# Where the columns and the weights of a matmul lie in SBUF, modulo 256 bytes, and three 128-column passes ahead of one tile

## The chip, the cores and the metric

The kernel runs on one core of one Trainium2 chip. The metric is device microseconds of one execution. Three executions of the kernel before took 2719.71, 2716.47 and 2715.73 us; the median is 2716.47 us.

## The reference

Two layers over 272 tokens (16 learned ones ahead of 256 of the input), width 2048. Cut to its matrix products:

```python
u = rmsnorm(h, norm_mix[0]);  h = h + ssd_mixer(u, ...)        # u @ in_proj, scan, g @ out_proj
h = h + swiglu(rmsnorm(h, norm_ffn[0]), gate_up[0], down[0])
kv = rmsnorm(h, kv_norm) @ w_kv
u = rmsnorm(h, norm_mix[1]);  h = h + stick_breaking_attention(u, w_q, k, v, w_o)
h = h + swiglu(rmsnorm(h, norm_ffn[1]), gate_up[1], down[1])
return rmsnorm(h, final_norm)[:, 16:]

def swiglu(u, w_gate_up, w_down):
    gu = u @ w_gate_up
    return (silu(gu[..., :5632]) * gu[..., 5632:]) @ w_down
```

Layer 0 and the shared keys and values need all 272 tokens; the queries and all that follows them need 256.

## The kernel before

**Tiling.** Activations stand transposed: 128 features on the partitions, tokens along the free axis (272, or 256 from the queries on). A projection is made one output tile at a time: 128 output features, accumulated in one PSUM bank over the K tiles of its input (16 for `u`, `ukv`, `uq` and `ob`; 8 for `y`, the half of the mixer's output that one call takes; 44 for `hid`). For each K tile the weights are a 128x128 block, loaded into TensorE, and the tokens are streamed past it.

**Three products per K tile.** Weights and activations are each split into a high part that the fp32r format holds and a low rest. `mac` (L107 to L112) issues for each K tile `wh*xh` (L110), `wh*xl` (L111) and `wl*xh` (L112); each is one weight load and one pass of 272 or 256 columns. The load for the next pass runs while the columns of the present one are read. So what is read from SBUF at the same time is always the columns of one pass and the weights of the pass behind it.

**How the weights come.** `load` (L91) fetches eight K tiles of a weight matrix (512 KB) into one of five `raw` buffers on SP's queue; `halves` (L99) makes `hi` on ScalarE (L101, five buffers) and `lo` on VectorE (L103, four buffers). `project` runs one output tile through that, `project_block` several output tiles in turn for each eight K tiles. Where an output tile is finished, VectorE reads it from PSUM (`times`, `residual`), and `split_scaled` writes the high and low part of the next input.

**Where things lie.** The tiles come from pools that fill each partition from low to high addresses. As the built program has it, in bytes of a partition:

| tile | starts at | modulo 256 | order inside | bytes from one K tile to the next |
|---|---|---|---|---|
| `hi`, `lo` (all buffers) | 81920 ... 114688 | 0 | K tile, 128 columns | 512 |
| `u`, `ukv` (272 columns) | 26624 | 0 | K tile, (high, low), token | 2176 (128 modulo 256) |
| `u` of layer 1 (256 columns) | 26624 | 0 | the same | 2048 (0 modulo 256) |
| `y` (272) | 132672, 150080 | 64 | the same | 2176 |
| `hid` of layer 0 (272) | 126400 | 192 | the same | 2176 |
| `hid` of layer 1, `uq`, `ob` (256) | 126400, 126400, 159168 | 192 | the same | 2048 |

In what follows, the distance of a pass is the address of the weights that are loaded meanwhile less the address of its columns, modulo 256. With 256 columns it is the same in every pass: 0 where the columns are those of `u`, 64 where they are those of `hid`, `uq` or `ob`. With 272 columns a high part is 1088 bytes long (64 modulo 256) and a K tile 2176, so the distance goes through 0, 192, 0, 128, 64, 128 over two K tiles of `u`, and through 64, 0, 64, 192, 128, 192 over those of `hid`.

**Stages**, in us from the span's start: `w_first`, `w_dt` and the mixer (272 columns, with the scan's small matmuls spread among the projections by `pump`) to 749; gate and up of layer 0 (272) to 1280; down (272) to 1543; keys, values and queries with the attention between (272 and 256) to 1863; `w_o` (256) to 1955; gate and up of layer 1 (`u`, 256) to 2462; down (`hid`, 256) to 2702; the final norm.

Of the kernel before, what the change touches and what calls it, by code (L numbers as in the profile page):

```python
# [29 lines left out]
WC = 8  # L30
# [7 lines left out]
WAKE = 10  # L38
RAW = 5
# [3 lines left out]
def trunk(tc, a, out):  # L43
# [3 lines left out]
    with tc.tile_pool(name="const", bufs=1) as cp, \  # L47
# [36 lines left out]
        uid = [0]  # L84

# [12 lines left out]

        def halves(raw, n, m=P):  # L99
            hi = wp.tile([P, WC, P], F32R, tag="hi", name=nm("hi"), bufs=5)  # L100
            S.copy(hi[:, :n, :m], raw[:, :n, :m])  # L101
            lo = wp.tile([P, WC, P], F32R, tag="lo", name=nm("lo"), bufs=4)
            V.tensor_tensor(out=lo[:, :n, :m], in0=raw[:, :n, :m],  # L103
                            in1=hi[:, :n, :m].bitcast(F32), op=ALU.subtract)
            return hi, lo

        def mac(ps, hi, lo, j, x, k, first, last, m=P):  # L107
            n = x.shape[-1]
            wh, wl, xh, xl = hi[:, j, :m], lo[:, j, :m], x[:, k, 0, :], x[:, k, 1, :]
            PE.matmul(ps[:, :n], wh, xh, start=first, stop=False)  # L110
            PE.matmul(ps[:, :n], wh, xl, start=False, stop=False)  # L111
            PE.matmul(ps[:, :n], wl, xh, start=False, stop=last)  # L112

        def project(src, x, m=P, o=None, then=None):
            K = x.shape[1]
            if o is None:
                o = pp.tile([P, 512], F32, tag="pp", name=nm("pp"))
            o = o[:m]
            for k0 in range(0, K, WC):
                c = min(WC, K - k0)  # L120
                if k0 % LC == 0:
                    raw = load(src, k0, min(LC, K - k0), m)
                hi, lo = halves(raw[:, k0 % LC:], c, m)
                for j in range(c):
                    mac(o, hi, lo, j, x, k0 + j, k0 + j == 0, k0 + j == K - 1, m)
                if k0 == 0 and then:
                    then()
            return o

        def project_block(srcs, x, then=None):  # L130
            K = x.shape[1]
            pss = [pp.tile([P, 512], F32, tag="pp", name=nm("pp")) for _ in srcs]
            for k0 in range(0, K, WC):
# [16 lines left out]
        def split_scaled(dst, k, src, gcol):  # L150
            S.activation(dst[:, k, 0, :], src, AF.Identity, scale=gcol)
            V.scalar_tensor_tensor(out=dst[:, k, 1, :], in0=src, scalar=gcol,
                                   in1=dst[:, k, 0, :].bitcast(F32),
                                   op0=ALU.mult, op1=ALU.subtract)
# [33 lines left out]
        u = upool.tile([P, KD, 2, T], F32R, tag="u", name="u0")  # L188
# [23 lines left out]
        with tc.tile_pool(name="ssd0", bufs=1) as q0, \  # L212
# [12 lines left out]
            ybuf = [q0.tile([P, 2 * GT, 2, T], F32R, name=f"y{i}") for i in range(2)]  # L225
# [113 lines left out]
            def ssd_scan(g, bc, xc, zs):  # L339
# [37 lines left out]
                ef = q2.tile([P, GT, T - OQ], F32, tag="ef", name=nm("ef"))  # L377
# [36 lines left out]
                ga = sp.tile([P, T], F32, tag="ga", name=nm("ga"))  # L414
# [20 lines left out]
                rg = sp.tile([P, T], F32, tag="rg", name=nm("rg"))  # L435
                rstd(rg, ga, DI // G)
                yield
                yb = ybuf[g // 2 % 2][:, g % 2 * GT:(g % 2 + 1) * GT]
                for j in range(GT):
# [3 lines left out]
                    S.copy(yb[:, j, 0, :], zs[:, j, :])  # L443
                    V.tensor_tensor(out=yb[:, j, 1, :], in0=zs[:, j, :], in1=yb[:, j, 0, :].bitcast(F32),
# [23 lines left out]
            u = upool.tile([P, KD, 2, T], F32R, tag="u", name="u1")  # L468
            out_project(6, u)


        def ffn(layer, u, t0, finish):
            n = T - t0
            with tc.tile_pool(name=f"ffn{layer}", bufs=1) as fp, \
                    tc.tile_pool(name=f"fft{layer}", bufs=2) as ft:
                hid = fp.tile([P, KF, 2, n], F32R, name=f"hid{layer}")
# [4 lines left out]
                for m in range(KF):  # L481
                    gt = ft.tile([P, n], F32, tag="gt", name=nm("gt"))
                    times(gt, pre.pop(0) if pre else project(gu[m], u), r)
# [4 lines left out]
                    S.copy(hid[:, m, 0, :], ut)  # L488
                    V.tensor_tensor(out=hid[:, m, 1, :], in0=ut, in1=hid[:, m, 0, :].bitcast(F32),
# [8 lines left out]
        def finish0(m, ps):  # L498
            if m == 0:
                ukv[0] = upool.tile([P, KD, 2, T], F32R, tag="u", name="ukv")  # L500
# [8 lines left out]
        with tc.tile_pool(name="att1", bufs=1) as b1p, \  # L509
                tc.tile_pool(name="att2", bufs=2) as b2p, \  # L510
                tc.tile_pool(name="psa", bufs=3, space=PSUM) as pap:
            uq = b1p.tile([P, KD, 2, SEQ], F32R, name="uq")
            for k in range(KD):
                split_scaled(uq, k, h[:, k, META:], gam[:, 1, k:k + 1])
            ob = b1p.tile([P, KD, 2, SEQ], F32R, name="ob")
# [17 lines left out]
            def attend(m, kT, vT, qT):  # L533
# [39 lines left out]
                S.copy(ob[:, m, 0, :], po[:, :SEQ])  # L573
                V.tensor_tensor(out=ob[:, m, 1, :], in0=po[:, :SEQ], in1=ob[:, m, 0, :].bitcast(F32),
# [21 lines left out]
            u = upool.tile([P, KD, 2, SEQ], F32R, tag="u", name="u2")  # L596
# [29 lines left out]
        diag = cp.tile([P, 2, P], F32, name="diag")  # L626
# [88 lines left out]
```

## Time and profile before

| | us |
|---|---|
| median of three runs | 2716.47 |
| the profiled execution, its own time | 2715.76 |
| its span (first to last instruction) | 2714.0 |
| VectorE busy in the span | 1605.6 |
| ScalarE busy | 1307.1 |
| DMA q1, share of 16 engines | 57.3% |
| granted TensorE clock, mean | 0.998 |

The profiled execution's own time is 1.8 us over its span and 0.7 us under the median. TensorE's busy time says little by itself, since a pass is recorded from its start to the end of its drain and neighbours overlap: a 272-column pass is shown with 287 ns, while the next one starts some 125 ns after it. The pace is read from the starts of the passes, or from their number in a stretch without pauses.

### The profile page before, as it was taken

Reading aid. Unit: us, or ns where it says so; the run is one execution under the profiler, and the core shown is the slowest. Engines: PE = TensorE matmul, PEld = TensorE weight load, DVE = VectorE, ACT = ScalarE, POOL = GpSimd, SP = SyncE. Lnnn points to the kernel's source line nnn. Section 1 sums busy time; section 2 is a strip of 40 time slices with the busy share of each in tenths; the row PEclk is TensorE's granted clock in tenths of the full one; section 3 lists DMA queues with packets and bytes.
Section 4 is the critical chain, followed back from the end, with each engine's and each line's share of the span. In section 5 each row is a group of like instructions: output and inputs, shape, how many; then the busy total and the mean of one; then the engine's idle time right before and its main releaser. Section 6 shows DMA issues by size and latency. Waiting matters only on the chain.

```text
span 2714.0 us, 52235 instructions
## 1 busy us (share of the span) xinstructions
PE 2700.6 (100%) x22112; PEld 2685.5 (99%) x22112; DVE 1605.6 (59%) x2220; ACT 1307.1 (48%) x1792; POOL 5.5 (0%) x22
## 2 busy tenths in 40 slices
PE   9999999999999999999999999999999999999998
PEld 9999999999999999999999999999999999999998
DVE  8777767668755555555444655555655555554554
ACT  7766566645544444444343544444544444443443
POOL 0000000000000000000000000000000000000000
PEclk9999999999999999999999999999999999999999
DMA  6755555654555555555555555555665666565664
GB/s 224 225 177 177 177 171 177 180 170 155 173 177 174 176 172 177 174 176 175 172 175 174 173 172 158 156 156 162 193 181 184 182 186 181 185 182 177 204 195 138
DMA packets 156235, 481.24 MB, mean 177 GB/s; under 512 B 18720, under 2 KB 39776, under 8 KB 156000
## 3 DMA queue, kind: packets, MB, share of 16 engines
q1 hardware_dynamic: 155712, 477.62, 57.3%
q8 instruction: 173, 2.83, 0.4%
q14 instruction: 62, 0.51, 0.1%
q10 hardware_dynamic: 288, 0.28, 0.0%
HBM read 475.67 MB, written 2.17 MB: 176 GB/s over the span
## 4 chain that ended last, share of the span: by engine, by line
PE 99%; DVE 0%; DMA 0%; ACT 0%; issue 0%; DVEq 0%; SPq 0%; ACTq 0%
PE pp L110 31%; PE pp L112 31%; PE pp L111 31%; PE py L422 1%; PE py L424 1%; PE pt L349 0%; PE po L571 0%; PE po L570 0%; PE psc L545 0%; PE pr L170 0%; DMA et<-cumD 0%; DMA raw<-w_first 0%; PE pe L110 0%; PE pe L112 0%; PE pe L111 0%; DVE o L642 0%
## 5 line engine op out<-in xcount | busy, mean ns | idle before, releaser
L101 ACT CAST hi<-raw 128x1024 fp32r<-128x1024 f32 (+1 forms) x899 | 928.5, 1034 | 1231.2 <-PE pp L111 994.9
L103 DVE TENSOR_TENSOR lo<-raw,hi 128x1024 fp32r<-128x1024 f32 (+1 forms) x899 | 1076.4, 1199 | 502.3 <-PE pp L112 280.9
L110 PE MATMUL pp<-u,hi 128*128 128x272 f32 (+1 forms) x4064 | 1166.7, 287 | 0.5 <-ACT hi L101 0.5
L112 PE MATMUL pp<-u,lo 128*128 128x272 f32 (+1 forms) x4064 | 1165.3, 287 | 0.2 <-DVE lo L103 0.2
L111 PE MATMUL pp<-u,hi 128*128 128x272 f32 (+1 forms) x4064 | 1163.2, 286 | 0.0
L111 PEld LDWEIGHTS pp<-u,hi 128*128 128x128 f32 x4064 | 775.3, 191 | 0.2
L110 PEld LDWEIGHTS pp<-u,hi 128*128 128x128 f32 x4064 | 769.4, 189 | 1.2 <-ACT hi L101 0.7
L112 PEld LDWEIGHTS pp<-u,lo 128*128 128x128 f32 x4064 | 768.9, 189 | 1.2 <-DVE lo L103 0.8
L110 PE MATMUL pp<-hid,hi 128*128 128x272 f32 (+1 forms) x1408 | 397.0, 282 | 0.0
L112 PE MATMUL pp<-hid,lo 128*128 128x272 f32 (+1 forms) x1408 | 396.4, 282 | 0.0
L111 PE MATMUL pp<-hid,hi 128*128 128x272 f32 (+1 forms) x1408 | 396.1, 281 | 0.0
L111 PEld LDWEIGHTS pp<-hid,hi 128*128 128x128 f32 x1408 | 265.3, 188 | 0.0
L110 PEld LDWEIGHTS pp<-hid,hi 128*128 128x128 f32 x1408 | 264.6, 188 | 0.0
L112 PEld LDWEIGHTS pp<-hid,lo 128*128 128x128 f32 x1408 | 264.3, 188 | 0.0
L110 PE MATMUL pp<-ukv,hi 128*128 128x272 f32 x512 | 149.0, 291 | 0.0
L110 PE MATMUL pp<-y,hi 128*128 128x272 f32 x512 | 148.7, 290 | 0.0
L112 PE MATMUL pp<-ukv,lo 128*128 128x272 f32 x512 | 147.6, 288 | 0.0
L111 PE MATMUL pp<-y,hi 128*128 128x272 f32 x512 | 147.4, 288 | 0.0
L111 PE MATMUL pp<-ukv,hi 128*128 128x272 f32 x512 | 147.4, 288 | 0.0
L112 PE MATMUL pp<-y,lo 128*128 128x272 f32 x512 | 147.1, 287 | 0.0
L145 DVE TENSOR_TENSOR gt<-pp,rB 128x272 f32<-128x272 f32 (+1 forms) x88 | 38.1, 433 | 145.0 <-PE pp L112 145.0
L145 DVE TENSOR_TENSOR ut<-pp,rB 128x272 f32<-128x272 f32 (+1 forms) x88 | 38.1, 433 | 144.0 <-PE pp L112 144.0
(218 smaller groups left out, 2602.2 us busy)
## 6 DMA issues: line engine op xcount, KB each, us to landing
raw<-w_gu SPq DMA_DIRECT2D x352, 512.0 KB, 3.6
raw<-w_down SPq DMA_DIRECT2D x160, 512.0 KB, 3.8
raw<-w_in SPq DMA_DIRECT2D x152, 512.0 KB, 3.6
raw<-w_out SPq DMA_DIRECT2D x64, 512.0 KB, 3.7
raw<-w_kv SPq DMA_DIRECT2D x64, 512.0 KB, 3.6
raw<-w_q SPq DMA_DIRECT2D x32, 512.0 KB, 3.6
raw<-w_o SPq DMA_DIRECT2D x32, 512.0 KB, 3.6
raw<-w_down SPq DMA_DIRECT2D x32, 256.0 KB, 2.6
```

Source lines behind the costliest of these rows:

```text
L101: S.copy(hi[:, :n, :m], raw[:, :n, :m])
L103: V.tensor_tensor(out=lo[:, :n, :m], in0=raw[:, :n, :m], in1=hi[:, :n, :m].bitcast(F32), op=ALU.subtract)
L110: PE.matmul(ps[:, :n], wh, xh, start=first, stop=False)
L111: PE.matmul(ps[:, :n], wh, xl, start=False, stop=False)
L112: PE.matmul(ps[:, :n], wl, xh, start=False, stop=last)
L145: V.tensor_tensor(out=dst, in0=ps[:, :r.shape[-1]], in1=r, op=ALU.mult)
L422: PE.matmul(py[i * HD:(i + 1) * HD, c0:c1], xd[b][:, 2 * j + i, :], gm[b][:, 2 * j + i, :], start=b < 2, stop=b != 1)
L424: PE.matmul(py[:, T:T + T - OQ], xw[:, 2 * j:2 * j + 2, :], cb[:, OQ:T], start=True, stop=True)
```

## The change

**Layout of the columns.** `pair` replaces the tile of (K tile, high or low, token) by one tile that holds all low parts and behind them, after a gap, all high parts; `PAD` sets what lies ahead. **Layout of the weights.** `hi` and `lo` are tiles of 1152 columns; with 272 tokens the K tiles of weights lie 144 columns (576 bytes, 64 modulo 256) apart, with 256 tokens 128 columns, and then `lo` begins 48 columns in. **Order in `mac`:** `wh*xl`, `wh*xh`, `wl*xh`. **Room:** `ef`, `ga` and `rg` have one buffer in place of two; `diag` stands in another pool. **Short passes:** ahead of the gate tile `m == 2` of layer 1, `syncopate` issues three passes of 128 columns into a PSUM bank that nothing reads.

As the built program has it, `hi` now starts at 64 and `lo` at 128 modulo 256 (192 more where it begins 48 columns in, so 64), the low parts of `u`, `y`, `uq`, `ob` and `hid` at 0, their high parts at 64 with 272 columns and at 0 with 256. The distance is 64 in every pass but some hundred of `w_first`.

```diff
+PAD = {"u": 0, "u2": 0, "y": 48, "uq": 16, "ob": 0, "hid": (16, 16)}
...
+        for tag, bufs in (("raw", RAW), ("hi", 5)):
+            wp.tile([P, 8 * P if tag == "raw" else WC * 144], F32 if tag == "raw" else F32R, tag=tag, name=f"{tag}_", bufs=bufs)
+        wp.tile([P, 16], F32, name="gap")
...
         def halves(raw, n, m=P):
-            hi = wp.tile([P, WC, P], F32R, tag="hi", name=nm("hi"), bufs=5)
+            st = STEP[0]
+            hi = wp.tile([P, WC * 144], F32R, tag="hi", name=nm("hi"), bufs=5)
+            hi = hi[:, :WC * st].rearrange("p (k c) -> p k c", c=st)
+            lo = wp.tile([P, WC * 144], F32R, tag="lo", name=nm("lo"), bufs=4)
+            o = 0 if st > P else 48
+            lo = lo[:, o:o + WC * st].rearrange("p (k c) -> p k c", c=st)
             S.copy(hi[:, :n, :m], raw[:, :n, :m])
-            lo = wp.tile([P, WC, P], F32R, tag="lo", name=nm("lo"), bufs=4)
...
+        def pair(pool, K, n, pad, gap, **kw):
+            t = pool.tile([P, pad + 2 * K * n + gap], F32R, **kw)
+            return [t[:, o:o + K * n].rearrange("p (k t) -> p k t", t=n) for o in (pad + K * n + gap, pad)]
+
         def mac(ps, hi, lo, j, x, k, first, last, m=P):
-            n = x.shape[-1]
-            wh, wl, xh, xl = hi[:, j, :m], lo[:, j, :m], x[:, k, 0, :], x[:, k, 1, :]
-            PE.matmul(ps[:, :n], wh, xh, start=first, stop=False)
-            PE.matmul(ps[:, :n], wh, xl, start=False, stop=False)
+            n = x[0].shape[-1]
+            wh, wl, xh, xl = hi[:, j, :m], lo[:, j, :m], x[0][:, k, :], x[1][:, k, :]
+            PE.matmul(ps[:, :n], wh, xl, start=first, stop=False)
+            PE.matmul(ps[:, :n], wh, xh, start=False, stop=False)
             PE.matmul(ps[:, :n], wl, xh, start=False, stop=last)
...
+            STEP[0] = 144 if x[0].shape[-1] == T else P
...
-        u = upool.tile([P, KD, 2, T], F32R, tag="u", name="u0")
+        u = pair(upool, KD, T, PAD["u"], 16, tag="u", name="u0")
...
-                ef = q2.tile([P, GT, T - OQ], F32, tag="ef", name=nm("ef"))
+                ef = q2.tile([P, GT, T - OQ], F32, tag="ef", name=nm("ef"), bufs=1)
...
+        def syncopate(x):
+            def short(hi, lo):
+                b = prp.tile([P, 512], F32, tag="pr", name=nm("beat"))
+                for w, s in ((hi, 0), (hi, 1), (lo, 0)):
+                    PE.matmul(b[:, :P], w[:, 0, :], x[s][:, 0, :P], start=True, stop=True)
+            return short
...
-                hid = fp.tile([P, KF, 2, n], F32R, name=f"hid{layer}")
+                hid = pair(fp, KF, n, PAD["hid"][layer], 16 * (1 - layer), name=f"hid{layer}")
...
+                    beat = syncopate(u) if (layer, m) == (1, 2) else None
+                    times(gt, pre.pop(0) if pre else project(gu[m], u, before=beat), r)
```

Three places in the order of the instructions. On TensorE, the end of the last tile of layer 1's first block and the beginning of the gate tile `m == 2` (`pp_2906`); before:

```order
L111 MATMUL pp_2874_22246<-u2_21128,hi_2899_22464 128x256
L112 MATMUL pp_2874_22246<-u2_21128,lo_2900_22466 128x256
L110 MATMUL pp_2906_22509<-u2_21128,hi_2908_22512 128x256 [waits DVE_49,Activation_49]
L111 MATMUL pp_2906_22509<-u2_21128,hi_2908_22512 128x256
L112 MATMUL pp_2906_22509<-u2_21128,lo_2909_22514 128x256
```

and in the changed kernel:

```order
L128 MATMUL pp_2874_22249<-u2_21131,hi_2899_22467 128x256
L129 MATMUL pp_2874_22249<-u2_21131,lo_2900_22468 128x256
L497 MATMUL beat_2910_22519<-u2_21131,hi_2908_22515 128x128 [waits Activation_49]
L497 MATMUL beat_2910_22519<-u2_21131,hi_2908_22515 128x128
L497 MATMUL beat_2910_22519<-u2_21131,lo_2909_22516 128x128 [waits DVE_49]
L127 MATMUL pp_2906_22512<-u2_21131,hi_2908_22515 128x256 [waits DVE_49]
L128 MATMUL pp_2906_22512<-u2_21131,hi_2908_22515 128x256
L129 MATMUL pp_2906_22512<-u2_21131,lo_2909_22516 128x256
```

Three passes of 128 columns stand ahead of the tile, and the wait for the tile's `lo` comes two passes ahead of its first full pass.

On TensorE at the start of the program, the first passes of `w_first` (`pp_1` to `pp_3`); before:

```order
L110 MATMUL pp_1_103<-u0_102,hi_6_122 128x272 [waits Activation_49]
L111 MATMUL pp_1_103<-u0_102,hi_6_122 128x272 [waits DVE_49]
L110 MATMUL pp_2_104<-u0_102,hi_6_122 128x272
L111 MATMUL pp_2_104<-u0_102,hi_6_122 128x272
L112 MATMUL pp_1_103<-u0_102,lo_7_124 128x272 [waits DVE_49]
```

and in the changed kernel:

```order
L127 MATMUL pp_1_106<-u0_105,hi_6_125 128x272 [waits DVE_49,Activation_49]
L128 MATMUL pp_1_106<-u0_105,hi_6_125 128x272
L127 MATMUL pp_2_107<-u0_105,hi_6_125 128x272
L128 MATMUL pp_2_107<-u0_105,hi_6_125 128x272
L129 MATMUL pp_1_106<-u0_105,lo_7_126 128x272 [waits DVE_49]
```

The low part of the columns is read first now, so the first pass waits for VectorE as well as for ScalarE.

On SP's queue, the load of the second scan's `ef` (it is read by `L406` and `L426` of that scan) among the loads of weights; before:

```order
L96 DMA raw_163_1392<-w_in 128x1024 [waits DMAHW6_49,DVE_49]
L361 DMA elast1_731<-cumD_469 16x8x16 [waits Pool_49]
L380 DMA ef_235_1920<-cumD_469 64x4x144
L380 DMA ef_235_1920<-cumD_469 64x4x144 [waits DMAHW7_49]
L96 DMA raw_169_1433<-w_in 128x1024 [waits DMAHW0_49,DVE_49]
```

and in the changed kernel:

```order
L382 DMA et_342_2730<-cumD_472 128x8x128 [waits PE_49]
L382 DMA elast0_733<-cumD_472 16x8x16 [waits PE_49]
L98 DMA raw_246_1990<-w_in 128x1024 [waits DMAHW6_49,DVE_49,Activation_49]
L401 DMA ef_235_1923<-cumD_472 64x4x144 [waits DMAHW7_49,DVE_49]
L401 DMA ef_235_1923<-cumD_472 64x4x144 [waits DMAHW0_49]
L98 DMA raw_252_2037<-w_in 128x1024 [waits DMAHW1_49,DVE_49,Activation_49]
```

With one buffer the load waits for VectorE's last reading of the scan before, and stands 16 rows later on the queue, still among loads of weights.

More of the change, by code (lines that the diff above doesn't have):

```diff
@@ L84, in trunk @@
         uid = [0]
+        STEP = [144]
         def nm(s):
@@ L123, in project @@
                 hi, lo = halves(raw[:, k0 % LC:], c, m)
+                if k0 == 0 and before:
+                    before(hi, lo)
                 for j in range(c):
@@ L130, in project_block @@
         def project_block(srcs, x, then=None):
-            K = x.shape[1]
+            K = x[0].shape[1]
             pss = [pp.tile([P, 512], F32, tag="pp", name=nm("pp")) for _ in srcs]
+            STEP[0] = 144 if x[0].shape[-1] == T else P
             for k0 in range(0, K, WC):
@@ L224, in trunk @@
             wT = q0.tile([P, NH], F32, name="wT")
-            ybuf = [q0.tile([P, 2 * GT, 2, T], F32R, name=f"y{i}") for i in range(2)]
+            ybuf = [pair(q0, 2 * GT, T, PAD["y"], 16, name=f"y{i}") for i in range(2)]
             with tc.tile_pool(name="dtp", bufs=1) as dq:
@@ L487, in ffn @@
                     V.tensor_tensor(out=ut, in0=ut, in1=gt, op=ALU.mult)
[L488 to L489 removed]
+                    S.copy(hid[0][:, m, :], ut)
+                    V.tensor_tensor(out=hid[1][:, m, :], in0=ut, in1=hid[0][:, m, :].bitcast(F32),
                                     op=ALU.subtract)
@@ L499, in finish0 @@
             if m == 0:
-                ukv[0] = upool.tile([P, KD, 2, T], F32R, tag="u", name="ukv")
+                ukv[0] = pair(upool, KD, T, PAD["u"], 16, tag="u", name="ukv")
             residual(h[:, m, :], ps)
```

35 lines of the change are left out of this document (17 added, 18 removed).

## The prediction

> **What bounds the kernel now.** I read the page's shares first, then the chain of work that ended last, then the number of passes in stretches of time, then single starts.
>
> ```profile
> span 2714.0 us, 52235 instructions
> PE 2700.6 (100%) x22112; PEld 2685.5 (99%) x22112; DVE 1605.6 (59%) x2220; ACT 1307.1 (48%) x1792; POOL 5.5 (0%) x22
> PE 99%; DVE 0%; DMA 0%; ACT 0%; issue 0%; DVEq 0%; SPq 0%; ACTq 0%
> PE pp L110 31%; PE pp L112 31%; PE pp L111 31%; PE py L422 1%; PE py L424 1%; PE pt L349 0%; PE po L571 0%; PE po L570 0%; PE psc L545 0%; PE pr L170 0%; DMA et<-cumD 0%; DMA raw<-w_first 0%; PE pe L110 0%; PE pe L112 0%; PE pe L111 0%; DVE o L642 0%
> ```
>
> TensorE is on the chain for 99% of the span, and the three lines of `mac` are 93% of it. It waits for nobody. So the time is the number of passes times the pace of one, and only the pace can change here. The waits say that the others have room:
>
> ```profile
> ACT hi L101 <- PE pp L111: 994.9, 652, 3.4
> DVE lo L103 <- PE pp L112: 280.9, 228, 2.4
> ...
> SPq L96 <- DVE lo L103: 1935.6, 756, 8.2
> ```
>
> ScalarE waits 995 us for TensorE to free a `hi` buffer, VectorE 281 us for a `lo` buffer, and SP's queue 1936 us for a `raw` buffer. Weights are ready early throughout.
>
> The pace, from the number of passes in four stretches (columns: us busy and number of instructions per engine): gate and up of layer 0, down of layer 0, gate and up of layer 1, down of layer 1.
>
> ```profile
> core 0: us, PE busy (x) PEld busy (x) DVE busy (x) ACT busy (x) POOL busy (x), PEclk, DMA share, GB/s
> 830.00:1275.00 445.00, 445.00 (x3546) 445.00 (x3545) 236.20 (x296) 183.58 (x222) 0.00 (x0) 1.00 0.57 176
> 1285.00:1540.00 255.00, 255.00 (x2045) 255.00 (x2044) 121.28 (x137) 101.96 (x123) 0.00 (x0) 1.00 0.58 176
> 1960.00:2455.00 495.00, 495.00 (x4126) 494.95 (x4125) 273.51 (x345) 214.99 (x261) 0.00 (x0) 1.00 0.60 183
> 2465.00:2700.00 235.00, 235.00 (x2076) 235.00 (x2075) 113.82 (x122) 102.18 (x123) 0.00 (x0) 1.00 0.59 180
> ```
>
> 445 us / 3546 is 125.5 ns a pass on `u` with 272 columns; 255 / 2045 is 124.7 on `hid` with 272; 495 / 4126 is 120.0 on `u` with 256; 235 / 2076 is 113.2 on `hid` with 256. The clock is 1.00 in all four. The last two are the same instruction with the same sizes at the same clock, nearly 7 ns apart. Single starts give it sharper, by lines of TensorE's timeline, first `u` with 272, then `u` with 256, `hid` with 256, and the first query tile `uq` with 256:
>
> ```profile
> 1000.06 0.29 PE L110 MATMUL pp<-u,hi 128*128 128x272 f32 x1
> ...
> 1002.32 0.29 PE L110 MATMUL pp<-u,hi 128*128 128x272 f32 x1
> ...
> 2199.84 0.28 PE L110 MATMUL pp<-u,hi 128*128 128x256 f32 x1
> ...
> 2201.64 0.28 PE L110 MATMUL pp<-u,hi 128*128 128x256 f32 x1
> ...
> 2600.00 0.28 PE L110 MATMUL pp<-hid,hi 128*128 128x256 f32 x1
> ...
> 2601.70 0.28 PE L110 MATMUL pp<-hid,hi 128*128 128x256 f32 x1
> ...
> 1555.67 0.28 PE L110 MATMUL pp<-uq,hi 128*128 128x256 f32 x1
> ...
> 1560.97 0.28 PE L110 MATMUL pp<-uq,hi 128*128 128x256 f32 x1
> ```
>
> 18 passes in 2.26 us: 125.6 ns. 15 in 1.80: 120.0. 15 in 1.70: 113.3. And 45 in 5.30 us: 117.8. So with 256 columns there are three steady paces: 120.0 where the distance is 0, and 113.3 or 117.8 where it is 64. With 272 columns, where the distance changes from pass to pass, it is 125.6 (124.7 on `hid`).
>
> That a load has a hand in it can be read from loads of half the size:
>
> ```profile
> L110 PEld LDWEIGHTS pp<-hid,hi 128*128 128x128 f32 x1408 | 264.6, 188 | 0.0
> L110 PEld LDWEIGHTS pt<-u,hi 128*64 128x64 f32 x16 | 2.1, 134 | 0.0
> ```
>
> 64 weight columns fewer take 54 ns less, so 128 of them are read for about 107 ns: a load reads SBUF for nearly the whole of a pass beside it, and the place of both has time to matter.
>
> **The change part by part.** The numbers of passes, from the groups of L110 kept apart by shape (L111 and L112 have the same numbers):
>
> ```profile
> L110 PE MATMUL pp<-u,hi 128*128 128x272 f32 x2656 | 768.1, 289 | 0.5 <-ACT hi L101 0.5
> L110 PE MATMUL pp<-u,hi 128*128 128x256 f32 x1408 | 398.6, 283 | 0.0
> L110 PE MATMUL pp<-hid,hi 128*128 128x272 f32 x704 | 202.6, 288 | 0.0
> L110 PE MATMUL pp<-hid,hi 128*128 128x256 f32 x704 | 194.3, 276 | 0.0
> L110 PE MATMUL pp<-ukv,hi 128*128 128x272 f32 x512 | 149.0, 291 | 0.0
> L110 PE MATMUL pp<-y,hi 128*128 128x272 f32 x512 | 148.7, 290 | 0.0
> L110 PE MATMUL pp<-uq,hi 128*128 128x256 f32 x256 | 72.2, 282 | 0.0
> L110 PE MATMUL pp<-ob,hi 128*128 128x256 f32 x256 | 71.2, 278 | 0.0
> L110 PE MATMUL pe<-u,hi 128*128 128x272 f32 x32 | 9.2, 288 | 0.0
> L110 PE MATMUL pt<-u,hi 128*64 128x272 f32 x16 | 4.8, 299 | 0.0
> ```
>
> *1. `u` of layer 1 (256 columns).* 3 x 1408 = 4224 passes go from distance 0 to 64. At 113.3 in place of 120.0 each, that is 4224 x 6.7 = **28.3 us less**. Bounds: at 117.8 it is 4224 x 2.2 = 9.3 us.
>
> *2. All passes of 272 columns.* 3 x 704 = 2112 on `hid`, and 3 x (2656 + 512 + 512 + 32 + 16) = 11,184 others, 13,296 in all. No row shows 272 columns at a constant distance of 64. Two ways from 113.3: by the share of columns, 113.3 x 272 / 256 = 120.4; by what 16 more columns cost on `u`, 125.6 - 120.0 = 5.6, so 118.9. I take **120.0**, near the first. Then 11,184 x 5.6 = 62.6 us and 2112 x 4.7 = 9.9 us, together **72.5 us less**. Bounds: at best the 16 columns more cost nothing, 113.3 (11,184 x 12.3 + 2112 x 11.4 = 161.6 us); at worst the pace keeps the 4.5 ns of `uq`'s second pace, 120.0 + 4.5 = 124.5 (11,184 x 1.1 = 12.3 us and 2112 x 0.2 = 0.4, together 12.7).
>
> *3. `hid` of layer 1, `uq`, `ob`.* Distance 64 before and after, only the place moves (192 to 0). Nothing, as long as the distance is what counts; the other case is a rival.
>
> *4. The three short passes.* On TensorE's path, each under a pass of 256 columns: at most 3 x 0.12 = 0.36 us added. What they could do is shift the pace of part 1: `uq` has 117.8 in its first tile, where it follows passes of 272 columns directly. I take +0.35.
>
> *5. Order in `mac`, and the first pass waiting for the low part.* At the start VectorE's first split is over at 3.77 + 0.50 us, while the first pass starts at 5.40, when `hi` is there:
>
> ```profile
> 3.77 0.50 DVE L152 SCALAR_TENSOR_TENSOR u<-h,gam,u 128x272 fp32r<-128x272 f32 x1 [2.51 <-ACT u L151]
> ...
> 5.40 0.37 PE L110 MATMUL pp<-u,hi 128*128 128x272 f32 x1
> ```
>
> Nothing. In later tiles the low part was written long before.
>
> *6. One `ef` buffer.* The load now waits for VectorE's last use in the scan before, and `raw` loads stand behind it on SP's queue, for which ScalarE's and VectorE's splits wait and then TensorE. Before, the load came out after that use in any case:
>
> ```profile
> 328.96 0.30 DVE L431 TENSOR_TENSOR yt<-yt,ef 128x144 f32<-128x144 f32 x1
> ...
> 330.23 0.58 SPq L380 DMA_DIRECT2D ef<-cumD  x1
> ...
> raw<-w_in SPq DMA_DIRECT2D x152, 512.0 KB, 3.6
> ```
>
> And five `raw` buffers of eight K tiles each are 5 x 24 x 125 ns = 15 us of passes. Zero; if that cover were gone, one landing of 3.6 us for each of seven scans, 25 us.
>
> *7. Splits written with a step of 144.* ScalarE and VectorE write eight pieces of 128 columns. The same work in one piece:
>
> ```profile
> L101 ACT CAST hi<-raw 128x1024 fp32r<-128x1024 f32 x863 | 906.4, 1052 | 1190.6 <-PE pp L111 969.3 <-issue 211.6 <-PE pp L112 3.7
> L103 DVE TENSOR_TENSOR lo<-raw,hi 128x1024 fp32r<-128x1024 f32 x863 | 1051.6, 1220 | 444.8 <-PE pp L112 227.2 <-issue 202.5 <-ACT hi L101 6.3
> ```
>
> 10% more would be some 90 and 105 us of busy time, beside 995 us that ScalarE waits for TensorE. Zero, and not below.
>
> Sum, against the profiled execution's own 2715.76 us (its span is 2714.0, the median 0.7 us above it): 2715.8 - 28.3 - 72.5 + 0.35 = 2615.3. I predict **2616 us** for the median.
>
> **The rivals.**
>
> *The 117.8 pace takes hold.* For it: `uq`'s first tile sits at 117.8 through 46 passes at a distance of 64 and does not leave it. Against: `hid` holds 113.3 for 235 us, entered from `u` without a pause. If the 272-column passes stay at 124.5 and `u` gets 113.3: 2715.8 - 12.7 - 28.3 = 2675. If both stay slow: 2715.8 - 12.7 - 9.3 = 2694. If only `u` of layer 1 does: 2715.8 - 72.5 - 9.3 = 2634.
>
> *The extra columns hide under the load.* If 113.3 is the load's own pace (107 ns of reading and a few more), 272 columns could cost half of 6.7 more, 116.7: 11,184 x 8.9 + 2112 x 8.0 = 116.4, so 2715.8 - 116.4 - 28.3 = 2571; with nothing more, 2526. The Trainium skill, "TensorE: Matmul & The Clock Gate", section "Back-to-back issue gap", states N / 2.4 + 2.5 ns for a pass by itself, so 109 and 116 ns by estimate; the trace's 113.3 for 256 columns is over the first of them.
>
> *The layout does nothing.* If columns and loads are read through ports that do not touch, 120.0 against 113.3 comes from something else of the stage, and all stays: 2716. The Trainium skill, "SBUF — State Buffer", section "Who interferes with whom", says just that: TensorE has two independent read ports, one for moving columns and one for weight loads, and never waits on anyone. The trace speaks against it: VectorE is busy for 274 of 495 us in the 120.0 stretch and for 114 of 235 in the 113.3 one, 55% against 48%, ScalarE for 43% in both; work that comes and goes like that would not make a pace that is one and the same over 15 and over 4126 passes.
>
> *The columns' own place counts, not the distance (slower).* Before, all weights lie at 0 modulo 256, so 113.3 goes with columns at 192 as much as with a distance of 64; the profile can't part them. After, `hid` of layer 1, `uq` and `ob` lie at 0, where `u` had 120.0. Then 3 x (704 + 256 + 256) = 3648 passes lose 6.7 ns, 24.4 us, and `u` wins nothing: 2740. It decides at the first query tile.
>
> **How the numbers follow.** My forecast 0.45; the 117.8 pace, whole or in part, 0.27; hidden columns 0.14; no effect 0.05; the place of the columns 0.09. The likeliest gives 2616. The range reaches up to the end of the 117.8 pace, 2695, and down to 2550, which takes in half of the hidden columns; the rest, some 0.2, lies outside. Faster by over 0.2% (5.4 us, about what a measurement of this kernel can tell from no change) is 0.86, within it 0.05, slower 0.09.
>
> **What would show it.** The number of passes in a stretch of gate and up of layer 0: 120 ns a pass, 3708 in 445 us. The same in layer 1: 113.3. `hid` of layer 1 unchanged at 113.3; were it 120, the place counts. 124 to 125 ns with 272 columns would be the kin of 117.8. DVE or SP's queue on the chain, or ScalarE's wait for a DMA, would show parts 6 or 7 wrong.

## The result, and the profile after

| | us | ratio to the kernel before, 95% interval |
|---|---|---|
| before, median of four runs | 2716.11 | |
| after, median of four runs (2696.40 to 2697.68) | 2697.14 | 0.9927, 0.9915 to 0.9939 |
| predicted | 2616 | |

The change makes the kernel faster, by 19 us and not by 100. The profiled execution took 2697.68 us.

The page of the kernel after, shares first:

```profile
span 2696.0 us, 52245 instructions
PE 2682.1 (99%) x22115; PEld 2666.8 (99%) x22115; DVE 1603.4 (59%) x2220; ACT 1307.2 (48%) x1792; POOL 5.5 (0%) x22
PE 99%; DVE 0%; DMA 0%; ACT 0%; issue 0%; DVEq 0%; SPq 0%; ACTq 0%
```

TensorE bounds it as before; only its pace can have changed. The passes in stretches of time (columns: us, busy us and number of instructions per engine): gate and up of layer 0, down of layer 0, gate and up of layer 1, down of layer 1.

```profile
core 0: us, PE busy (x) PEld busy (x) DVE busy (x) ACT busy (x) POOL busy (x), PEclk, DMA share, GB/s
830.00:1275.00 445.00, 445.00 (x3531) 445.00 (x3530) 234.98 (x294) 181.94 (x221) 0.00 (x0) 1.00 0.57 174
1285.00:1540.00 255.00, 255.00 (x2024) 255.00 (x2024) 121.88 (x139) 100.88 (x123) 0.00 (x0) 1.00 0.56 173
2000.00:2420.00 420.00, 420.00 (x3709) 420.00 (x3708) 241.55 (x309) 191.21 (x232) 0.00 (x0) 1.00 0.64 194
2465.00:2680.00 215.00, 215.00 (x1900) 215.00 (x1899) 105.01 (x114) 94.80 (x116) 0.00 (x0) 1.00 0.58 179
```

126.0 ns a pass with 272 columns in both stages of layer 0, where it had been 125.5 and 124.7; 113.2 in both stages of layer 1, where gate and up had 120.0. One or two passes at the edges of a stretch are counted with it, so steady paces below come from the starts of single passes in the trace. By these the stages changed so:

| stretch | passes | ns from start to start, before | after | change, us |
|---|---|---|---|---|
| `u` of layer 1, 256 columns | 4224 | 120.04 | 113.40 | -28.0 |
| `u` of the mixer, 272 | 3840 | 127.17 | 127.72 | +2.1 |
| `y`, 272 | 1536 | 126.7 | 127.1 | +0.7 |
| `u` of layer 0, gate and up, 272 | 4224 | 125.60 | 126.16 | +2.4 |
| `hid` of layer 0, 272 | 2112 | 124.82 | 126.11 | +2.7 |
| `ukv`, 272 | 1536 | 126.37 | 127.01 | +1.0 |
| `uq`, `ob`, `hid` of layer 1, 256 | 3648 | 114.4 | 114.4 | 0.0 |

The sum is -19.1; with 0.4 for the small matmuls of the final norm (`prow`, first start to last: 0.44 us before, 0.80 after) and 0.3 for the short passes it is -18.4, and the span is 18.0 shorter. The groups by shape and the waits show the same, beside those of before:

```profile
L127 PE MATMUL pp<-u,hi 128*128 128x272 f32 x2656 | 769.0, 290 | 0.5 <-ACT hi L114 0.5
...
L127 PE MATMUL pp<-u,hi 128*128 128x256 f32 x1408 | 388.9, 276 | 0.0
...
L127 PE MATMUL pp<-hid,hi 128*128 128x256 f32 x704 | 194.3, 276 | 0.0
```

```profile
ACT hi L114 <- PE pp L128: 982.6, 656, 3.2
DVE lo L115 <- PE pp L129: 284.2, 229, 2.3
```

One pass of `u` with 256 columns went from 283 ns to the 276 of `hid`; one with 272 from 289 to 290. ScalarE and VectorE wait for TensorE nearly as long as before.

### The profile page after: what moved, and what is told of

Same layout as the page of the kernel before. It is cut to its first block, busy times and chain, and to the rows that moved or that the text cites. A ratio compares the mean times of both kernels' runs of the same rounds, so it can differ in the third digit from the quotient of the medians.

```text
span 2696.0 us, 52245 instructions
## 1 busy us (share of the span) xinstructions
PE 2682.1 (99%) x22115; PEld 2666.8 (99%) x22115; DVE 1603.4 (59%) x2220; ACT 1307.2 (48%) x1792; POOL 5.5 (0%) x22
## 4 chain that ended last, share of the span: by engine, by line
PE 99%; DVE 0%; DMA 0%; ACT 0%; issue 0%; DVEq 0%; SPq 0%; ACTq 0%
PE pp L128 31%; PE pp L127 31%; PE pp L129 31%; PE py L443 1%; PE py L445 1%; PE pt L370 0%; PE po L601 0%; PE po L600 0%; PE psc L575 0%; PE pr L191 0%; DMA et<-cumD 0%; DMA raw<-w_first 0%; PE pe L128 0%; PE pe L127 0%; PE pe L129 0%; DVE o L672 0%
## 5 line engine op out<-in xcount | busy, mean ns | idle before, releaser
L114 ACT CAST hi<-raw 128x1024 fp32r<-128x1024 f32 (+1 forms) x899 | 928.3, 1034 | 1211.8 <-PE pp L128 982.6
L115 DVE TENSOR_TENSOR lo<-raw,hi 128x1024 fp32r<-128x1024 f32 (+1 forms) x899 | 1076.9, 1199 | 494.6 <-PE pp L129 284.2
L129 PE MATMUL pp<-u,lo 128*128 128x272 f32 (+1 forms) x4064 | 1151.3, 284 | 0.0
L128 PEld LDWEIGHTS pp<-u,hi 128*128 128x128 f32 x4064 | 764.1, 188 | 0.2
L127 PEld LDWEIGHTS pp<-u,hi 128*128 128x128 f32 x4064 | 762.9, 188 | 1.1 <-ACT hi L114 0.7
```

The costliest lines, as they stand in the source:

```text
L115: V.tensor_tensor(out=lo[:, :n, :m], in0=raw[:, :n, :m], in1=hi[:, :n, :m].bitcast(F32), op=ALU.subtract)
L127: PE.matmul(ps[:, :n], wh, xl, start=first, stop=False)
L128: PE.matmul(ps[:, :n], wh, xh, start=False, stop=False)
```

## The experiments

### Without the short passes

```diff
-                    beat = syncopate(u) if (layer, m) == (1, 2) else None
+                    beat = None
```

> The changed kernel without the three short passes. Theory A (the passes are idle weight, since the trace of after has 113 to 114 ns a pass on u of layer 1 before them as well as behind them): 0.3 to 0.4 us faster than after, 2696.8 us, with 113.3 ns on u of layer 1 throughout. Theory B (they hold the pace): u of layer 1 falls to 117.8 ns from its gate tile 2 on, 4000 passes x 4.5 ns = 18 us slower, 2715 us.

Ten executions: eight took 2726.7 to 2727.8 us, two 2696.0 and 2696.9; the median is 2727.42, the ratio to before 1.0013 (0.9981 to 1.0045). The profiled one, of 2727.76 us, by the same kind of stretches (`ob`, then gate and up, then down of layer 1):

```profile
1884.00:1955.00 71.00, 71.00 (x602) 70.89 (x601) 43.30 (x63) 34.90 (x51) 0.00 (x0) 1.00 0.59 179
2000.00:2420.00 420.00, 420.00 (x3569) 420.00 (x3568) 234.92 (x298) 183.61 (x223) 0.00 (x0) 1.00 0.61 187
2465.00:2680.00 215.00, 215.00 (x1827) 215.00 (x1827) 102.77 (x110) 91.27 (x110) 0.00 (x0) 1.00 0.60 184
```

All three go at 117.7 to 118 ns. The layout is that of the change, and `hid` at this distance had 113.3 before. So the same code at the same addresses has two paces, and in this execution the one that the attention leaves in `ob` stays through 6300 passes, over every tile's edge and the pause for `rstd`, to the end. From the starts: 4224 x (117.82 - 113.40) + 2112 x (117.78 - 113.33) = 18.7 + 9.4, and 3.1 in `ob`: 31.2 us; the medians lie 30.3 apart.

Not all of that is the short passes'. `ob` lies ahead of them, so its 3.1 us are not theirs, nor the first 192 passes of `u`: what they can save in an execution in which `ob` ends at 117.8 is 4032 x 4.42 + 2112 x 4.45 = 27.2 us. And `ob` ended at 113.3 in the profiled execution of the change, and by their times in its three others; by the times of the two executions at 2696, 113.3 then holds without short passes too. Which pace `ob` has differs between executions: of the twelve traces of this case, in seven it ends at 113.3 and in five at 117.8. What decides it is not shown.

### The distance of `u` of layer 1 alone

The kernel before, with that one tile moved by 192 bytes.

```diff
-            u = upool.tile([P, KD, 2, SEQ], F32R, tag="u", name="u2")
+            u = upool.tile([P, 48 + KD * 2 * SEQ], F32R, tag="u", name="u2")
+            u = u[:, 48:].rearrange("p (k s t) -> p k s t", s=2, t=SEQ)
```

> The kernel before, with one thing changed: u of layer 1 begins 192 bytes later in its buffer, so that the distance of its 256-column passes is 64 in place of 0. Theory A (the 256-column gain is the distance alone, and what the change does to the passes of 272 columns is a loss): u of layer 1 at 113.3 ns, all else as before, 2716.1 - 28 = 2688 us, 9 us under after. Theory B (it needs the new order of the halves or the new place of the weights as well): 120.0 or 117.8 ns on u, 2707 to 2716 us.

2715.75 us, ratio 0.9997 (0.9988 to 1.0007): no difference. `ob`, gate and up, and down of layer 1:

```profile
1885.00:1955.00 70.00, 70.00 (x597) 70.00 (x596) 45.25 (x67) 35.95 (x53) 0.00 (x0) 1.00 0.60 187
2000.00:2420.00 420.00, 420.00 (x3568) 420.00 (x3568) 234.49 (x297) 182.90 (x223) 0.00 (x0) 1.00 0.61 186
2465.00:2680.00 215.00, 215.00 (x1828) 215.00 (x1827) 103.16 (x111) 91.97 (x112) 0.00 (x0) 1.00 0.60 186
```

117.8 again. Gate and up win 4224 x (120.04 - 117.82) = 9.4 us, and down, which before had 113.3 behind the 120.0 stretch, loses 2112 x (117.78 - 113.34) = 9.4. The right distance by itself is worth nothing here. The time lies in the range that was expected if more of the change were needed, but that is not the reason, as the next run shows.

In the profiled execution, of 2718.83 us, `ob` ended at 117.8, and `u` kept that. Seven of the ten took 2714.9 to 2716.0, some 3 us less, which is what lies between the two paces of `ob`. So `ob` probably ended at 113.3 in them, and `u` took 117.8 even so; no trace shows one of these. If so, the pace is not always the one of the stage before.

### That distance and the short passes, without the rest

The kernel of the last experiment, with `syncopate` and its call as in the change.

> The kernel before, with u of layer 1 moved by 192 bytes (distance 0 to 64) and the three short passes ahead of a tile of layer 1. Nothing else of the change: 272-column passes, halves, weights and order of passes stay as before. Theory A (distance 64 allows two steady paces, 113.3 and 117.8; which one holds is carried over from the passes before, and the three short passes set it to 113.3): ob may enter at 117.8 or 113.3, u of layer 1 has 113.3 behind the short passes and down of layer 1 stays at 113.3, the 272-column stretches keep 125.6 and 124.8: 2715.8 - 28.0 + 0.3, so 2688, and 2692 at most, in every run. Rival B (the 113.3 of the change hangs on another part of it: the order of the passes, weights with a step of 144, the halves kept apart): u of layer 1 stays at 117.8 behind the short passes, and down of layer 1 too where ob enters at 117.8: 2706 to 2728.

2688.71 us (2688.30 to 2691.26), ratio 0.9900 (0.9883 to 0.9916); 2688 was expected. In the profiled execution `ob` came in at 117.8 ns, so one sees the turn. TensorE's timeline around the short passes (`beat`; x2 is two passes in a row):

```profile
1979.41 0.28 PE L110 MATMUL pp<-u,hi 128*128 128x256 f32 x1
...
1980.11 0.28 PE L110 MATMUL pp<-u,hi 128*128 128x256 f32 x1
1980.23 0.28 PE L111 MATMUL pp<-u,hi 128*128 128x256 f32 x1
1980.35 0.28 PE L112 MATMUL pp<-u,lo 128*128 128x256 f32 x1
1980.47 0.33 PE L478 MATMUL beat<-u,hi 128*128 128x128 f32 x2
1980.64 0.28 PE L478 MATMUL beat<-u,lo 128*128 128x128 f32 x1
1980.75 0.34 PE L110 MATMUL pp<-u,hi 128*128 128x256 f32 x1
1980.92 0.28 PE L111 MATMUL pp<-u,hi 128*128 128x256 f32 x1
1981.04 0.28 PE L112 MATMUL pp<-u,lo 128*128 128x256 f32 x1
```

And the passes in the stretches ahead of it, behind it, and in down of layer 1:

```profile
1885.00:1955.00 70.00, 70.00 (x597) 70.00 (x596) 44.85 (x67) 35.65 (x54) 0.00 (x0) 1.00 0.61 186
2000.00:2420.00 420.00, 420.00 (x3709) 420.00 (x3707) 242.22 (x310) 191.50 (x232) 0.00 (x0) 1.00 0.63 194
2450.00:2670.00 220.00, 220.00 (x1943) 220.00 (x1942) 108.84 (x118) 97.95 (x119) 0.00 (x0) 1.00 0.58 183
```

117.3 ahead, 113.2 behind and to the end. From the first short pass to the first full one it is 0.28 us, and that full pass lasts from 0.75 to 0.92. After some six more passes the pace is 113.3, and by their times all four executions have it, where none of the ten without the short passes had. So neither the order of the halves nor the new place of the weights is needed for 113.3. This kernel is 8 us faster than the changed one, since its 272-column passes keep the paces of before.

### What of the short passes does it

The changed kernel, with the weights of each gate tile of layer 1 moved to one of five other distances, and ahead of the up tile, which has the distance of the change, a number of passes of some width.

```diff
+                for w, s in ((hi, 0), (hi, 1), (lo, 0), (hi, 0), (hi, 1), (lo, 0))[:count]:
+                    PE.matmul(b[:, :cols], w[:, 0, :], x[s][:, 0, :cols], start=True, stop=True)
```

> The changed kernel with a test of the short passes at each m from 2 to 41 of layer 1. The gate tile has its weights moved (five different distances, none of which holds 113.3), the up tile has the distance 64 of the change, and ahead of it stand 0 short passes, 1, 2 or 3 of 128 columns, 3 of 64, 3 of 192, 3 of full 256 columns, or 6 of 128; each with each of the five distances before. Theory A (two steady paces at distance 64; passes short enough that a load is alone for a while set it to 113.3): with 3 or 6 passes of 128 or 64 columns all up tiles go at 113.3; with none, or with 3 full ones, some go at 117.8 (the pace is what the distance before left), and 192 columns, which take 90 ns beside a load of 107, do as 128. Rival B (short passes are without effect; tiles take 113.3 by themselves as soon as the distance is right): the settings with none and with 3 full ones show 113.3 as often as the others.

Every up tile ends (mean of the last 24 starts) either at 113.33 or at 117.75 to 117.79:

| ahead of the tile | none | 1 x 128 | 2 x 128 | 3 x 128 | 3 x 64 | 3 x 192 | 3 x 256 | 6 x 128 |
|---|---|---|---|---|---|---|---|---|
| of five tiles at 113.3 | 3 | 3 | 4 | 5 | 3 | 4 | 3 | 4 |

Three full passes leave each of the five tiles at the pace that it has without them. Short ones move the pace, either way: one of 128 made the first tile slow that is fast without it. So the expectation that any short passes give 113.3 fell; what holds is that three of 128 did so from all five entries, as in the run before. That is no proof for every entry, and with three of five at 113.3 without short passes this table alone would not show that three of 128 do anything. The turn inside a trace, in the run before and in the next one, shows it. Why they turn the pace is open.

### How many columns, and how much load

Gate and up tiles with settings of their own for K tiles 1 to 14 (in layer 1 read with a step of 256 columns, so that all K tiles lie at one place modulo 256 and the distance is 64; in layer 0 the place moves by 64 bytes from K tile to K tile).

```diff
+                c = max(n, CUT[0][0]) if first else n if last else CUT[0][0]
+                m = m if first or last else CUT[0][1]
```

> The changed kernel, in which the gate and up tiles from m = 2 on stream another number of columns or load fewer weight columns in K tiles 1 to 14 (three m for each pair of numbers); the outputs of those tiles are therefore not the reference's. Distance 64 at the start of every pass. Theory A (remainder: with a number of columns that is no multiple of 64, that is of 256 bytes, columns and loads run into each other whatever the distance): in layer 0, 256 columns give 113.3 ns and 320 give 140.0 ((320 + 16) / 2.4), while 264, 272, 280, 288, 304 and 336 lie 4 to 6 ns over (columns + 16) / 2.4. Theory B (new place from K tile to K tile in layer 0 is what costs, not the number): 256 columns in layer 0 stay over 117 ns, and 272 columns in layer 1, where every K tile begins at the same place, give 120.0. Theory C (the columns' own stream, not the load, sets 126 ns at 272): 64 and 32 weight columns with 272 columns change nothing; if the load is at fault, 32 weight columns give 116 to 118 ns. With fewer than 256 columns in layer 1 the pace stays at 109 to 113 ns if the load limits it there.

Here too `ob` came in at 117.7, and the passes went from 117.7 to 113.34 at the short ones. Mean ns of the last 24 starts in layer 1, six tiles each:

| columns, with 128 weight columns | 256 | 264 | 272 | 288 | 304 | 320 |
|---|---|---|---|---|---|---|
| ns | 113.3 | 120.0 | 123.3 | 133.3 | 138.7 | 146.7 |

Eight columns more than 256 cost 6.7 ns and sixteen 10.0, where 113.3 x 16 / 256 is 7.1. With a half and a quarter of the weight columns, in layer 0, 272 columns took 124.6 and 125.0 ns: hardly less than the 126.1 with all of them.

The same run shows what the load does at a constant place and the distance 64. With 128 weight columns, 224, 192 and 128 columns all take 111.7 ns: there the load sets the pace (128 columns with 32 weight columns take 60.0). But 256 columns take 113.3 with 128, 64 or 32 weight columns. So 113.3 is not the load's pace but, at this place and distance, what 256 columns cost by themselves, and 16 columns more have to be paid. Of the theories, C comes nearest; A's 140.0 for 320 columns in layer 0 was 146.1, B's 120.0 for 272 in layer 1 was 123.3, and 256 in layer 0 took 115.0 and not over 117.

### The place of the load

Four scans with a setting for each tile. First the changed kernel with its weights moved in steps of 64 bytes, two or three m of each layer for each of 15 pairs of moves:

```diff
+            oh = 16 * OFF[0][0]
+            hi = hi[:, oh:oh + WC * st].rearrange("p (k c) -> p k c", c=st)
...
+            o = (0 if st > P else 48) + 16 * OFF[0][1]
```

> The changed kernel with four raw buffers in place of five and wider hi and lo buffers, in which hi and lo of the gate and up tiles from m = 2 on begin 0, 64, 128 or 192 bytes further on, in the 15 pairs but (0, 0), so that the distances of the loads of wh and of wl go through all pairs. Theory A (some distance is right for 272 columns, only not 64): one or more of the 15 pairs give 120 to 122 ns in layer 0. Theory B (remainder: no distance is right for 272): all 15 lie between 124 and 128 ns. In layer 1, with 256 columns: 113.3 ns for distances (64, 64), 120.0 for (0, 0), and the other pairs between or above, if the distance is what counts there.

With 272 columns the pairs gave 123.9 to 127.2 ns, none of them 120; with 256 columns the last 24 starts gave 113.3 to 120.0, entered from whatever came before. 113.3 stood there at two more pairs of distances: 64 for the high weights with 192 for the low ones, and the reverse. So the next scan put the short passes ahead of each gate tile:

> Gate and up tiles m = 2 to 43 of both layers, each m with a setting of its own, three short passes ahead of each gate tile, K tiles 1 to 14 only; the output is not the reference's. Layer 0 (rows of 272 columns, so the place moves by 64 bytes from K tile to K tile): 272 columns with the high weights moved by 0, 64, 128, 192 bytes and the low ones by 0 to 192, in two orders of the three passes; 256 columns; 16 weight columns. Layer 1 (272 columns read with a step of 256, so the place is the same in every K tile): the same 16 moves with 272 columns, then with 256; other orders; 64, 32 and 16 weight columns. Theory A (with 272 columns the place of the load is not what sets the pace): every one of the 272 settings lies at 123 to 128 ns, none at 120.5 or less, 16 and 32 weight columns too; at a constant place some 2.6 ns less than at a moving one, near 123.5. Rival C (272 columns have a 120.0 too, by the distance, but the change has the wrong distance for the low part, the wrong order or the wrong entry): one or more of the 16 moves, in one order or behind the short passes, holds 120.0, and small loads show 120.0 whatever the place.

TensorE's timeline has first two starts with 272 columns at a constant place and the distance 64, 10 K tiles (30 passes) apart. Then, for 256 columns, two starts in an up tile, 14 K tiles (42 passes) apart, at the distances 64, 128, 192 and 0, and at last two with 272 columns and 16 weight columns, 13 K tiles (39 passes) apart:

```profile
2001.22 0.41 PE L154 MATMUL pp<-u,hi 128*128 128x272 f32 x2
...
2004.92 0.41 PE L154 MATMUL pp<-u,hi 128*128 128x272 f32 x2
...
2197.67 0.39 PE L154 MATMUL pp<-u,hi 128*128 128x256 f32 x2
...
2202.43 0.39 PE L154 MATMUL pp<-u,hi 128*128 128x256 f32 x2
...
2255.47 0.40 PE L154 MATMUL pp<-u,hi 128*128 128x256 f32 x2
...
2260.45 0.40 PE L154 MATMUL pp<-u,hi 128*128 128x256 f32 x2
...
2313.57 0.40 PE L154 MATMUL pp<-u,hi 128*128 128x256 f32 x2
...
2318.51 0.40 PE L154 MATMUL pp<-u,hi 128*128 128x256 f32 x2
...
2372.01 0.40 PE L154 MATMUL pp<-u,hi 128*128 128x256 f32 x2
...
2377.05 0.40 PE L154 MATMUL pp<-u,hi 128*128 128x256 f32 x2
...
2468.05 0.41 PE L154 MATMUL pp<-u,hi 128*16 128x272 f32 x2
...
2472.91 0.41 PE L154 MATMUL pp<-u,hi 128*16 128x272 f32 x2
```

For 272 columns 3.70 us / 30 is 123.3. For 256, 4.76 us / 42 is 113.3 at 64; 118.6 at 128; 117.6 at 192; 120.0 at 0. With 256 columns the distance matters, in one kernel, side by side. Here the weights moved and the columns stayed; in the kernel before and in the two runs with its `u` moved by 192 bytes the weights stayed, and again 0 went with 120.0 and 64 with 113.3 or 117.8, so it is not the place of one of them alone. With 272 columns and an eighth of the load it is 4.86 / 39 = 124.6; with a half and a quarter 124.5 and 124.7. All other settings of 272 lay between 122.2 and 127.3: at a constant place 123.3 with the distance 64, and 126.7 with 128 and with 192; at the moving place of layer 0 the change's own setting 126.1, the best (low weights moved by 64 bytes) 123.9. At the moving place 256 columns at the distance 64 take 115.0 and not 113.3.

Two more scans moved a third thing, the high half of the columns, then the weights in steps of 32 bytes, and put passes into other places of PSUM.

> Gate and up tiles m = 2 to 43 of both layers, a setting of its own for each tile, K tiles 1 to 14 only; the output is not the reference's. In both layers first all 64 ways to put three things against the low half of the columns at 272 columns: high weights, low weights and high half of the columns, each moved by 0, 64, 128 or 192 bytes. Then at 272: passes that add to no sum, every second pass into another PSUM bank, PSUM places 16, 64 and 240; moves of 16 and 32 bytes; 16 weight columns with the high half moved; last 256 columns with 16 weight columns. Layer 0 has rows of 272 columns (the place moves by 64 bytes from K tile to K tile), layer 1 a step of 256. Theory A (272 columns cost some 123 to 127 ns by themselves, what the load adds is 3 ns at most): no way gives 120.5 or less; 16 weight columns stay at 124.5 whatever the place of the high half. Rival C (272 has a 120.0 that one right set of places reaches, which the kernel has not): one or more ways hold 120.0. Rival D (the sum in PSUM sets 272, because 272 columns pass a line there): another bank, another place in the bank or no sum gives 120.

> As in places, a setting for each gate and up tile, K tiles 1 to 14 only; the output is not the reference's. 272 columns, high and low weights each moved by 0 to 224 bytes in steps of 32 (64 ways; layer 0 with the moving place, layer 1 with the constant one), some moves of 16 bytes, and passes that go to two PSUM banks in turn without waiting. Theory A (272 columns have a lottery of paces from 122 to 127 and no 120.0): the moves of 32 bytes fill the same band; the best known in layer 0, high weights moved by 32 bytes, shows 122.7 to 123.3 again. Two banks: 123 to 126 as with one. Rival C: some move of 32 bytes holds 120.0. Rival D (the sum in one PSUM bank sets 272): 120.0 with two banks.

Some 300 settings with 272 columns: the lowest 122.2, the highest 128.9, none at 120. Another place in the PSUM bank doesn't bring 120 (126.2 at the moving place for two of them, 126.7 and 123.3 at the constant one), nor do two banks in turn (126.1 and 123.3, as with one). In the first of the two scans the passes into a second bank, those that add to no sum and those at place 16 waited for a tile, and say nothing. The 122.2 (constant place, high weights moved by 192 bytes and low ones by 128) is one of two paces: other tiles with this setting have 125.7 to 126.1. The best setting at the moving place is the high weights 32 bytes further on: 122.75 to 122.79 in the last 24 passes of each of three tiles. What makes it so is not explained: one setting with 16 weight columns (the high half moved by 64 bytes) has 122.8, the others 123.9 to 124.9, so less load is not always less time. Nor is the second pace at 256 columns tied to a whole load: in the first of the two scans, at a constant place and the distance 64, three tiles with 16 weight columns, behind tiles that waited, went at 117.7, where the scan with the short passes has 113.3.

### The version that the scan points to

The changed kernel with the high weights 32 bytes further on wherever the columns are 272:

```diff
             hi = hi[:, :WC * st].rearrange("p (k c) -> p k c", c=st)
+            hi = hi[:, :, 8:8 + P] if st > P else hi
```

> The changed kernel with one thing more: where the columns are 272, the high weights lie 32 bytes further on (distance 96 for them, 64 for the low ones). Layer 1 is as in the change. Theory A (with 272 columns each set of places has a pace of its own between 122 and 128, which holds in every stage alike since the distances are the same there): 122.75 ns in place of 126.1, as in the scan: 13,296 x 3.36 = 44.7 us less than the changed kernel, 2652; gate and up of layer 0 4224 x 122.75 = 518.5 us. Rival B (122.75 was one of several paces at these places, as 113.3 is at 256, and is not taken from every entry): part of the tiles stay at 125 to 126 and the times of single executions scatter over tens of us, between 2655 and 2697.

2657.05 us (2656.55 to 2657.97), ratio 0.9782 (0.9769 to 0.9795): 59 us faster than the kernel before, 40 faster than the changed one. The page, and the passes in gate and up and in down of layer 0:

```profile
span 2654.9 us, 52245 instructions
```

```profile
830.00:1230.00 400.00, 400.00 (x3260) 400.00 (x3259) 217.04 (x272) 167.97 (x204) 0.00 (x0) 1.00 0.58 179
1260.00:1500.00 240.00, 240.00 (x1958) 240.00 (x1957) 115.90 (x131) 97.39 (x118) 0.00 (x0) 1.00 0.57 177
```

122.7 and 122.6 ns. From the starts, gate and up of layer 0 take 122.84 x 4224 = 518.9 us, down 122.78 x 2112 = 259.3, 14.0 and 7.0 less than in the changed kernel. In the mixer and in `ukv`, where other matmuls stand between the tiles, the mean is 124.2 to 124.9, some 2.8 less than in the changed kernel and not 3.36: over 6912 passes that is 3.7 of the 5 us by which 2652 was missed. Most passes there go at 122.8 too; some tiles begin at 133, as in the changed kernel, and five of the 64 `y` tiles end at 125 or 126. That much of rival B is there, but single executions do not scatter: all five lie within 1.4 us.

## Why the prediction was wrong

**Part 1, `u` of layer 1: right.** 28.3 us were predicted, 28.0 measured, at the predicted 113.3. But the distance is only half of it. At 64 there is a second steady pace, 117.8, and without the short passes 18 of 20 executions of two kernels took it, by their times. That the four executions after the change had 113.3 is in part luck: `ob` ended at 113.3 in them.

**Part 2, 272 columns: the step that failed.** "I take **120.0**, near the first", 72.5 us less; the measured pace is 126.1, some 9 us more than before. The working took the pace at 256 columns and stretched it by the share of columns, 113.3 x 272 / 256, as if only their number counted and a right distance gave 272 columns the same gain as 256. The runs show two errors in it. At the distance 64 and a constant place 272 columns cost 123.3, not 120.0: 3.3 too few, and with half the weight columns or fewer it is no less, so it is not the length of the load. And a constant distance isn't a constant place: with rows of 1088 bytes the columns move by 64 bytes from K tile to K tile, and there the change's setting has 126.1, another 2.8. (With a moving place the distance is 64 in every pass only if the high half also lies 64 bytes from the low half; the runs do not part these two.) Together 6.1 x 13,296 = 81 us, which is the 72.5 that did not come and the 9 that were lost. The upper bound, 124.5, was 120.0 with the 4.5 of `uq`'s second pace, so it carried the same error. No row of before had a stretch of 272 columns under 124.7; the 120.0 rested on no row of that size.

**Part 3: right.** `hid` of layer 1, `uq` and `ob` have the same means as before at their new place.

**Part 4: the price was right, 0.3 us; the use was not seen.** "What they could do is shift the pace of part 1" was there, and was given no weight in the sum. In the profiled execution after the change it can't be seen: `ob` came in at 113.4 and the pace behind the short passes is the one ahead of them. The runs in which `ob` comes in at 117.8 show the use, some 27 us there.

**Parts 5 to 7: right, nothing.** ScalarE's wait for TensorE is 982.6 us in place of 994.9, VectorE's 284.2 in place of 280.9; DMA has 0% of the chain, as before. The 0.4 us of the final norm had no term.

**The rivals.** *The 117.8 pace takes hold*: real, and where it comes in, the short passes are what stands against it. Its 2694 for the case that both stay slow lies near the result, but by other terms: 256 columns got 113.3, and 272 lost. The argument against it, that `hid` enters 113.3 from `u` without a pause, held for 120.0 ahead of it and not for 117.8. *Extra columns hide under the load*: fell, 16 more cost 10; the load's own pace is 111.7, and 113.3 is already the columns'. *The layout does nothing*: fell at 256 columns, by 113.3 to 120.0 in one kernel. The Trainium skill, "SBUF — State Buffer", section "Who interferes with whom", calls TensorE's two reads independent; the 113.3 at one distance and the 120.0 at another do not agree with it. *The columns' own place counts*: fell for one place against another, but a place that moves from K tile to K tile costs 256 columns some 2 ns and 272 some 3.

## What to carry to other kernels

Where a pace is steady to a tenth of a ns but differs between stages, it may have more than one steady value for the same code and addresses, and the one that holds can be left over from the work before: take several executions, and look at the pace at a stage's entry, before a layout is called good or bad. A pace measured at one size says nothing sure of the next size; give each tile of a long loop its own setting and some hundred variants are measured in one run. Parts of a change that look like one idea should be run apart: here one part brought 28 us, one cost 9, and a third, at 0.3 us, decided in some executions whether the first came at all.

## What the hardware showed unexpectedly

- Passes of 256 columns at the distance 64 have two steady paces, 113.3 and 117.8 ns, each stable over thousands of passes; three passes of 128 columns turned 117.8 into 113.3 in both traces in which the passes ahead of them went at 117.8.
- Columns above 256 cost more than their share: 264 take 120.0 ns, 272 take 123.3 and 288 take 133.3, at a constant place and the distance 64, with the load of 128 columns unchanged. 256 columns at the faster of their paces take 113.3 with 128 weight columns and with 16.
- With 272 columns an eighth of the load still leaves 124.5 ns at most settings, while 32 bytes in the place of the high weights move it from 126.1 to 122.75. Why is open.
